# Later pools, four products ahead at a group boundary, one plain tile last, and another place for the forms of h, in a four-layer trunk

## The chip, the cores and the metric

The kernel runs on one core of a Trainium2 chip. The metric is the device time of one execution in microseconds (us); shown are the median of several runs and one profiled execution. TensorE is called PE, VectorE DVE, ScalarE ACT, GpSimd POOL; SP issues the transfers.

## The reference

A trunk of four post-norm layers on a sequence of 512 tokens of width 1024, all in float32. Each layer is a token mixer and a SwiGLU channel mixer (FFN) of 2816 hidden units:

```python
for i in range(DEPTH):
    x = sublayer(x, mixer[i % 4])      # mLSTM, sliding-window, HGRN2, differential attention
    x = sublayer(x, swiglu)            # (silu(h @ w_gate) * (h @ w_up)) @ w_out
# sublayer: h = x*(1+scale_c)+shift_c ; x = LayerNorm(alpha*x + (1+gate_c)*f(h))
```

The scale, shift and gate of each sub-layer are linear in one conditioning vector c.

## The kernel before

Activations lie transposed, features on the 128 partitions and 512 tokens in the free dimension; `xz` is the stream. A float32 product is made of three in the float32r type: each operand is split into a high part and the rest, and hi·hi, lo·hi and hi·lo are added in PSUM (`mm3`, L198 to L202; L502 for the Strassen products). A weight of 128 x 1024 is loaded into a `raw` buffer (L187), its high part `wh` is made by ACT (L190, L479) and the rest `wl` by DVE (L191, L480). `raw` has 7 buffers of 4 KB per partition, `wh` and `wl` 5 each, PSUM 8 banks.

The conditioning weights (`in_ada_w`, 192 loads of 512 KB) go through the same `raw` buffers. Each such column is one custom DVE instruction (L124). They are issued in between: each call of `weights` issues `rate` of them, unless `hold` counts down first (L192 to L195).

The FFN (L568 to L624) works in 22 hidden tiles of 128. Before, the first four are plain: their gate and up products use h itself (`hh`, `hl`). Between them `t_forms` (L458 to L473) makes four tiles `tf` of sums of h's blocks, which need the four blocks `H` in float32. The other 18 tiles are 9 pairs, each by one level of Strassen: seven products of 24 matmuls of 256 columns, on sums of weight blocks made in `raw` (L516, L542). Results are gathered by L513 to L564 and gated: silu and product by L528 and L554, split into `pair` by ACT (L555) and DVE (L556). After groups of 8, 8 and 6 hidden tiles comes an output projection of that group (`out_proj`, L322 and on): eight steps, one weight and one PSUM bank each, folded into `xz` by DVE (L337). The last one of a sub-layer runs its last four steps in two halves of the tokens, and the layer norm of the first half runs beside the second: sums S (L342 to L348), mean and variance by PE and DVE (L381, L388 to L398), scaling (L408, L416), then the next h (L444 ACT, L447 POOL, L448 DVE).

Each stage has its own pools in the memory that the stage before gives back: `tf`, `pairs` and `mid` for an FFN, `big` and `mid` for a mixer (`pools`, L66 to L74). Before, `run` opens them ahead of the generator of the stage. The code is a set of generators; the framework puts each engine's instructions into one fixed order when the kernel is built, by priority in the order of the code and by when it reckons inputs and buffers to be free. An engine works its own order strictly.

Addresses in a partition, from the built program: `wh` and `wl` lie at 1216 modulo 2048, `hh` and `hl` at 704, `tf` at 1216; all of these, and `pair`, at 64 modulo 128.

Of the kernel before, what the change touches and what calls it, by code (L numbers as in the profile page):

```python
# [19 lines left out]
P = 128  # L20
D = 1024
# [6 lines left out]
FGROUPS = (8, 8, 6)  # L28
FPLAIN = 4
# [13 lines left out]
class Trunk:  # L43
# [22 lines left out]
    def pools(self, kind):  # L66
# [368 lines left out]
    def modulate(self, z, hs, hb, k, t, eng=None):  # L435
# [3 lines left out]
        else:  # L439
            x = (k // 4, t.start // 256)  # L440
            if x not in self.keep:
                self.keep[x] = self.raw.tile([P, 4, 256], F32, tag="raw", name=self.nm("H"))
            h = self.keep[x][:, k % 4, :]
# [124 lines left out]
    def ffn(self, layer, gate):  # L568
# [12 lines left out]
        acts = []  # L581
        src = lambda j: [a["ffn_in"][layer, j, :, x, :] for x in range(2)]
# [7 lines left out]
        for x in (pa, pb):  # L590
            acts += [x[:, :, 0, :], x[:, :, 1, :]]
        n = (KF - FPLAIN) // 2
        steps = [None] * n

        def begin(i):
            if i < n:
                act = self.pair_tile()
                steps[i] = self.strassen(a["ffn_dp"][layer, i], forms, act), act
                next(steps[i][0])

        ends, j0 = np.cumsum(FGROUPS), 0
        begin(0)
        next(steps[0][0])
        for i in range(n):
            g, act = steps[i]
            for s in range(5):
                if s == 3:
                    begin(i + 1)
                if s == 4 and i + 1 < n:
                    next(steps[i + 1][0])  # L610
                next(g)
                yield 0.0
            acts += [act[:, :, 0, :], act[:, :, 1, :]]
            gn = len(acts)
            if j0 + gn in ends:
                srcs = [a["ffn_out"][layer, d, :, j0 * P : (j0 + gn) * P] for d in range(KD)]
                self.rate = 2
                if j0 + gn == KF:
# [238 lines left out]
    def swa(self, layer, gate):  # L857
        nc, a = self.nc, self.a
# [585 lines left out]
```

## Time and profile before

| | before |
|---|---|
| median of 3 runs | 2512.93 us (2512.45 to 2520.49) |
| the profiled execution | 2519.93 us, span 2517.9, mean granted clock 0.981 |
| PE busy | 2407.0 us, 96% of the span |
| DVE busy | 1811.3 us, 72% |
| PE waiting for ACT's first splits (L190) | 38.8 us in 6 times, 13.1 of it at the start |
| PE waiting for ACT's `pair` (L555) | 22.4 us in 9 times |

A row of the timeline is start, length, engine, line, operation, output and inputs, count, and in brackets the idle time before with what ended it. A row of the windows gives the window, its length, then busy time and count for PE, PE's weight loads, DVE, ACT and POOL, the granted clock, the transfers' share and GB/s. The four steps from a mixer to its FFN lie at about 244, 795, 1499 and 2141 us, the three from an FFN to the next mixer at 600 to 650, 1160 to 1200 and 1860 to 1900. The fourth FFN has no conditioning columns beside it.

### The profile page before, as it was taken

Reading aid. Unit: us, or ns where it says so; the run is one execution under the profiler, and the core shown is the slowest. Engines: PE = TensorE matmul, PEld = TensorE weight load, DVE = VectorE, ACT = ScalarE, POOL = GpSimd, SP = SyncE. Lnnn points to the kernel's source line nnn. Section 1 sums busy time; section 2 is a strip of 40 time slices with the busy share of each in tenths; the row PEclk is TensorE's granted clock in tenths of the full one; section 3 lists DMA queues with packets and bytes.
Section 4 is the critical chain, followed back from the end, with each engine's and each line's share of the span. In section 5 each row is a group of like instructions: output and inputs, shape, how many; then the busy total and the mean of one; then the engine's idle time right before and its main releaser. Section 6 shows DMA issues by size and latency. Waiting matters only on the chain.

```text
span 2517.9 us, 39980 instructions
## 1 busy us (share of the span) xinstructions
PE 2407.0 (96%) x15416; PEld 2148.6 (85%) x15416; DVE 1811.3 (72%) x3137; ACT 1104.9 (44%) x1917; POOL 476.9 (19%) x714
## 2 busy tenths in 40 slices
PE   7998999999998999997999989999989999899998
PEld 5777989898768989897888889898978888899997
DVE  6956887878786887877655567878785556866665
ACT  3543534343653635343433335343436554544443
POOL 5003100004334000006433331000042223200002
PEclk9999999999998999998999999999999999999999
DMA  8831373736210363744221103736362210332321
GB/s 311 291 127 42 118 243 92 243 101 201 76 35 26 118 234 92 243 142 151 84 68 60 51 29 123 234 99 237 117 196 85 66 43 26 109 118 84 118 80 47
DMA packets 93998, 312.31 MB, mean 124 GB/s; under 512 B 10736, under 2 KB 13168, under 8 KB 93808
## 3 DMA queue, kind: packets, MB, share of 16 engines
q1 hardware_dynamic: 92800, 309.43, 37.9%
q8 instruction: 121, 1.98, 0.3%
q14 instruction: 69, 0.57, 0.1%
q10 hardware_dynamic: 1008, 0.32, 0.1%
HBM read 307.62 MB, written 2.10 MB: 123 GB/s over the span
## 4 chain that ended last, share of the span: by engine, by line
PE 73%; DVE 13%; DMA 6%; issue 3%; POOL 2%; ACT 2%; ACTq 0%; DVEq 0%; POOLq 0%; SPq 0%
PE ps L502 18%; PE ps L200 15%; PE ps L202 15%; PE ps L201 15%; DMA raw<-in_ada_w 4%; DVE raw L124 3%; DVE wl L191 3%; DVE wl L480 2%; PE ps L1209 1%; PE ps L1043 1%; PE ps L905 1%; ACT wh L190 1%; PE ps L1270 1%; PE ps L1071 1%; DVE xz L408 1%
## 5 line engine op out<-in xcount | busy, mean ns | idle before, releaser
L479 ACT ACTIVATE wh<-raw 128x1024 fp32r<-128x1024 f32 x252 | 267.0, 1061 | 424.3 <-PE ps L502 161.6
L502 PE MATMUL ps<-tf,wh 128*128 128x256 f32 x2304 | 418.3, 283 | 0.5 <-ACT b L513 0.5
L190 ACT ACTIVATE wh<-raw 128x1024 fp32r<-128x1024 f32 (+1 forms) x251 | 256.1, 1029 | 318.0 <-PE ps L201 114.3
L480 DVE TENSOR_TENSOR wl<-raw,wh 128x1024 fp32r<-128x1024 f32 x252 | 307.6, 1223 | 110.7 <-ACT wh L479 110.6
L191 DVE TENSOR_TENSOR wl<-raw,wh 128x1024 fp32r<-128x1024 f32 (+1 forms) x251 | 302.5, 1212 | 110.2 <-ACT wh L190 92.0
L502 PEld LDWEIGHTS ps<-tf,wh 128*128 128x128 f32 x2304 | 359.8, 192 | 2.9 <-ACT b L513 2.3
L502 PE MATMUL ps<-tf,wl 128*128 128x256 f32 x1152 | 326.0, 283 | 0.0
L200 PE MATMUL ps<-pair,wh 128*128 128x512 f32 (+1 forms) x800 | 295.1, 370 | 22.4 <-ACT pair L555 22.4
L201 PE MATMUL ps<-pair,wh 128*128 128x512 f32 (+1 forms) x800 | 294.1, 369 | 0.0
L202 PE MATMUL ps<-pair,wl 128*128 128x512 f32 (+1 forms) x800 | 293.3, 368 | 0.0
L124 DVE CUSTOM_DVE_ANT_0 raw<-raw,cond,adab 128x1024 f32<-128x1024 f32 x192 | 255.7, 1344 | 48.6 <-DMA raw<-in_ada_w 48.5
L200 PE MATMUL ps<-hh,wh 128*128 128x256 f32 (+1 forms) x616 | 213.6, 352 | 38.4 <-ACT wh L190 37.6
L200 PE MATMUL ps<-wh,hh 128*128 128x512 f32 (+1 forms) x608 | 241.1, 399 | 6.5 <-ACT hh L444 5.1
L502 PE MATMUL ps<-hh,wl 128*128 128x256 f32 x864 | 244.5, 283 | 0.0
L502 PE MATMUL ps<-hl,wh 128*128 128x256 f32 x864 | 244.5, 283 | 0.0
L502 PE MATMUL ps<-hh,wh 128*128 128x256 f32 x864 | 244.5, 283 | 0.0
L337 DVE SCALAR_TENSOR_TENSOR xz<-ps,gate,xz 128x512 f32<-128x512 f32 (+1 forms) x208 | 129.6, 625 | 148.2 <-PE ps L202 147.4
L201 PE MATMUL ps<-wl,hh 128*128 128x512 f32 (+1 forms) x608 | 222.7, 366 | 1.7 <-DVE wl L191 1.6
L202 PE MATMUL ps<-wh,hl 128*128 128x512 f32 (+1 forms) x608 | 222.1, 365 | 0.6 <-DVE hl L448 0.6
L502 PEld LDWEIGHTS ps<-tf,wl 128*128 128x128 f32 x1152 | 221.1, 192 | 0.0
L201 PE MATMUL ps<-hl,wh 128*128 128x256 f32 (+1 forms) x616 | 212.8, 348 | 6.5 <-DVE hl L448 6.3
L202 PE MATMUL ps<-hh,wl 128*128 128x256 f32 (+1 forms) x616 | 213.4, 350 | 5.3 <-DVE wl L191 5.3
(290 smaller groups left out, 4978.2 us busy)
## 6 DMA issues: line engine op xcount, KB each, us to landing
raw<-in_ada_w SPq DMA_DIRECT2D x192, 512.0 KB, 4.7
raw<-in_ffn_dp SPq DMA_DIRECT2D x144, 512.0 KB, 3.7
raw<-in_ffn_out SPq DMA_DIRECT2D x64, 512.0 KB, 3.7
raw<-in_ffn_in SPq DMA_DIRECT2D x32, 512.0 KB, 3.9
raw<-in_ffn_out SPq DMA_DIRECT2D x32, 384.0 KB, 3.5
raw<-in_m_vo SPq DMA_DIRECT2D x16, 512.0 KB, 5.6
raw<-in_h_qf SPq DMA_DIRECT2D x16, 512.0 KB, 3.6
raw<-in_h_ig SPq DMA_DIRECT2D x16, 512.0 KB, 3.8
```

Source lines behind the costliest of these rows:

```text
L124: self.nc.vector.tensor_tensor_reduce(w, w, self.cond, 1.0, self.adab[:, sub, j : j + 1], ALU.mult, ALU.add, mod[:, j : j + 1])
L190: nc.scalar.activation(hi[:, :n], raw[:, :n], AF.Copy)
L191: (eng or nc.vector).tensor_tensor(lo[:, :n], raw[:, :n], hi[:, :n].bitcast(F32), ALU.subtract)
L200: nc.tensor.matmul(ps, lhs[0], rhs[0], start=start, stop=False)
L201: nc.tensor.matmul(ps, lhs[0], rhs[1], start=False, stop=False)
L202: nc.tensor.matmul(ps, lhs[1], rhs[0], start=False, stop=stop)
L337: nc.vector.scalar_tensor_tensor(z, ps[:, t], gate[:, d : d + 1], z, ALU.mult, ALU.add)
L408: V.tensor_tensor(z, z, st[:, 0, :], ALU.subtract)
L479: nc.scalar.activation(hi, raw, AF.Copy)
L480: nc.vector.tensor_tensor(lo, raw, hi.bitcast(F32), ALU.subtract)
L502: nc.tensor.matmul(ps[:, j * 256 : j * 256 + 256], w[a][:, c], m[b], start=first and j == k == a == b == 0, stop=k == 3 and a == 1, skip_g ...
L905: nc.tensor.matmul(ps, qTs[j][:, q], kz[:, :, k0 : k0 + nk * P], start=True, stop=True)
```

## The change

1. FGROUPS becomes (7, 8, 7). Three plain tiles stand at the head of an FFN; the fourth is the last hidden tile, made on PE between and behind the last pair's last products, and gated into a tile of its own.
2. At a group boundary two more products of the next pair run ahead of the output projection, four in all. The next pair's four loaded blocks keep four of the seven `raw` buffers through it.
3. The pools of a stage open inside the stage's generator: after 16 steps (the first half) of the FFN's first projection, after 7 or 8 steps of a mixer's. The mixers' rope tables and masks are issued behind that.
4. The four blocks `H` are allocated ahead of the mixer's last output projection; each gets a memset of one column on POOL.
5. `hold` is 8 for every stage but the first: no column is issued with its first eight weights.
6. In the FFN's memory the pairs come first, then 64 bytes (`off`, one memset), then `tf` and `mid`. `tf` is then at 0 modulo 128, `wh` and `wl` at 64.

The arithmetic is the same. 48 matmuls of 512 columns become 96 of 256, 64 weights of 1024 or 768 columns become 64 of 896; the loads are the same in number. POOL gets 20 memsets.

```diff
-FGROUPS = (8, 8, 6)
-FPLAIN = 4
+FGROUPS = (7, 8, 7)
+FPLAIN = (0, 1, 2, KF - 1)
...
         if kind == "ffn":
-            self.tf, self.pairs, self.mid = pool("tf", 4), pool("pairs", 4), pool("mid", 7)
+            self.pairs, off = pool("pairs", 4), pool("off", 1)
+            self.nc.gpsimd.memset(off.tile([P, 16], F32, name=self.nm("off")), 0.0)
+            self.tf, self.mid = pool("tf", 4), pool("mid", 7)
...
-        pa, pb = self.pair_tile(), self.pair_tile()
-        yield from self.proj_cols(
+        first = self.proj_cols(
             src(0) + src(1), "t", lambda ps: (gated(pa, 0, ps[0], ps[1]), gated(pa, 1, ps[2], ps[3]))
         )
+        for _ in range(2 * KD):
+            yield next(first)
+        self.pools("ffn")
+        pa, pb = self.pair_tile(), self.pair_tile()
+        yield from first
+        forms = self.t_forms()
         yield from self.proj_cols(src(2), None, lambda ps: gated(pb, 0, *ps))
-        forms = self.t_forms()
-        yield from self.proj_cols(src(3), None, lambda ps: gated(pb, 1, *ps))
...
+        cur = begin(0)
+        self.advance(cur[0], 2)
+        left = 5
         for i in range(n):
-            g, act = steps[i]
-            for s in range(5):
-                if s == 3:
-                    begin(i + 1)
-                if s == 4 and i + 1 < n:
-                    next(steps[i + 1][0])
-                next(g)
-                yield 0.0
+            g, act = cur
+            self.advance(g, left - 2)
+            yield 0.0
+            nxt = begin(i + 1) if i + 1 < n else None
+            if nxt:
+                self.advance(nxt[0], 1)
+            else:
+                last(0)
+            self.advance(g, 1)
+            if nxt:
+                self.advance(nxt[0], 1)
+            self.advance(g, 1)
+            yield 0.0
             acts += [act[:, :, 0, :], act[:, :, 1, :]]
+            if nxt is None:
+                last(1)
+                pc = self.pair_tile()
+                gated(pc, 0, *bank)
+                acts.append(pc[:, :, 0, :])
+            cur, left = nxt, 5
             gn = len(acts)
             if j0 + gn in ends:
...
+                self.advance(nxt[0], 2)
+                left = 3
                 yield from self.out_proj(srcs, 1, acts, gate, False)
...
     def swa(self, layer, gate):
         nc, a = self.nc, self.a
+        first = self.proj_tok(a["s_q"][0], 512, lambda *x: qdone(*x))
+        for _ in range(KD - 1):
+            yield next(first)
+        self.pools("mix")
         self.rope_tables()
...
-            if i:
-                self.pools(kind)
             gen = getattr(self, kind)(layer, gate)
...
-            self.rate, self.hold = 2 if kind == "mlstm" else 1, 0
+            self.rate, self.hold = 2 if kind == "mlstm" else 1, 8 if i else 0
...
-            self.keep = {} if more and plan[i + 1][0] == "ffn" else None
+            self.keep = None
+            if more and plan[i + 1][0] == "ffn":
+                blocks = [(x, y) for y in range(2) for x in range(2)]
+                self.keep = {b: self.raw.tile([P, 4, 256], F32, tag="raw", name=self.nm("H")) for b in blocks}
+                for x in self.keep.values():
+                    self.nc.gpsimd.memset(x[:, 0, 0:1], 0.0)
             out = self.out_proj(srcs, per, acts, gate, True)
```

Lines of the changed kernel are four or five higher up to the FFN: a split at L190 is L194 there, L444 is L445, L337 is L341, L124 is L128, L516 is L517, L554 to L556 are L555 to L557.

ACT at the first step from a mixer to its FFN. `sq` are the squares for the norm, `hh` the new h, `wh` the splits of the FFN's first weights. Before:

```order
L346 ACTIVATE sq_2045<-xz 128x256
L444 ACTIVATE hh<-xz,hb_1707,hs_1706 128x256 x2
L346 ACTIVATE sq_2072<-xz 128x256
L190 ACTIVATE wh_2097<-raw_2095 128x1024
L444 ACTIVATE hh<-xz,hb_1707,hs_1706 128x256
L190 ACTIVATE wh_2103<-raw_2101 128x1024
L190 ACTIVATE wh_2109<-raw_2107 128x1024
L190 ACTIVATE wh_2115<-raw_2113 128x1024
L444 ACTIVATE hh<-xz,hb_1707,hs_1706 128x256
```

After; one more split, of the first weight, stands ahead of all the squares, nine rows further up:

```order
L347 ACTIVATE S<-xz 128x256
L194 ACTIVATE wh_2096<-raw_2094 128x1024
L350 ACTIVATE sq_1917<-xz 128x256
L350 ACTIVATE sq_1947<-xz 128x256
L194 ACTIVATE wh_2102<-raw_2100 128x1024
L350 ACTIVATE sq_1965<-xz 128x256
L445 ACTIVATE hh<-xz,hb_1707,hs_1706 128x256
L350 ACTIVATE sq_1995<-xz 128x256
L194 ACTIVATE wh_2108<-raw_2106 128x1024
L445 ACTIVATE hh<-xz,hb_1707,hs_1706 128x256 x2
L350 ACTIVATE sq_2023<-xz 128x256
L194 ACTIVATE wh_2419<-raw_2417 128x1024
```

The splits moved from behind the last square to between the squares. Further down, not shown, the second weight of the third tile stands in the new order behind the four copies that make `tf`; before, there was a split ahead of these copies.

DVE at the first group boundary. `pair` is the pair that the coming output projection uses last, the rows on `raw` and `mod` are conditioning columns, `wl` the splits of its weights. Before:

```order
L124 ISA raw_3152,mod_2091<-raw_3152,cond,adab 128x1024
L124 ISA mod_2091 128x1
L556 TENSOR_TENSOR pair_2706<-b_434_2738,pair_2706 128x2x256
L191 TENSOR_TENSOR wl_3146<-raw_3143,wh_3145 128x1024
L516 TENSOR_TENSOR b_459_2967<-ps_3006,b_459_2967 128x512
L191 TENSOR_TENSOR wl_3184<-raw_3181,wh_3183 128x1024
L124 ISA raw_3187,mod_2091<-raw_3187,cond,adab 128x1024
L124 ISA mod_2091 128x1
L516 TENSOR_TENSOR b_447_2872<-ps_2878,b_447_2872 128x512
L124 ISA raw_3190,mod_2091<-raw_3190,cond,adab 128x1024
L124 ISA mod_2091 128x1
L554 SCALAR_TENSOR_TENSOR b_447_2872<-b_453_2932,b_447_2872 128x512
```

After:

```order
L557 TENSOR_TENSOR pair_2648<-b_427_2680,pair_2648 128x2x256
L517 TENSOR_TENSOR b_452_2909<-ps_2948,b_452_2909 128x512
L195 TENSOR_TENSOR wl_3106<-raw_3103,wh_3105 128x896
L128 ISA raw_3138,mod_2086<-raw_3138,cond,adab 128x1024
L128 ISA mod_2086 128x1
L517 TENSOR_TENSOR b_440_2814<-ps_2820,b_440_2814 128x512
L128 ISA raw_3141,mod_2086<-raw_3141,cond,adab 128x1024
L128 ISA mod_2086 128x1
L555 SCALAR_TENSOR_TENSOR b_440_2814<-b_446_2874,b_440_2814 128x512
L195 TENSOR_TENSOR wl_3135<-raw_3132,wh_3134 128x896
L557 TENSOR_TENSOR pair_2648<-b_440_2814,pair_2648 128x2x256
```

Of the columns that stood between the gathering of the last pair and its gating, two are left; the first gating stands ahead of them.

DVE at the last output projection of the first FFN, around the first half's folds (128x256) and the norm's sums S. Before:

```order
L337 SCALAR_TENSOR_TENSOR xz<-ps_5325,gate_1705,xz 128x512
L191 TENSOR_TENSOR wl_5702<-raw_5699,wh_5701 128x1024
L337 SCALAR_TENSOR_TENSOR xz<-ps_5385,gate_1705,xz 128x256
L124 ISA raw_5976,mod_2092<-raw_5976,cond,adab 128x1024
L124 ISA mod_2092 128x1
L337 SCALAR_TENSOR_TENSOR xz<-ps_5409,gate_1705,xz 128x256
L124 ISA raw_5985,mod_2092<-raw_5985,cond,adab 128x1024
L124 ISA mod_2092 128x1
L337 SCALAR_TENSOR_TENSOR xz<-ps_5433,gate_1705,xz 128x256
L337 SCALAR_TENSOR_TENSOR xz<-ps_5457,gate_1705,xz 128x256
L347 TENSOR_TENSOR S<-S,xz 128x256
L348 TENSOR_TENSOR S<-S,sq_5477 128x256
```

After:

```order
L341 SCALAR_TENSOR_TENSOR xz<-ps_5308,gate_1705,xz 128x512
L195 TENSOR_TENSOR wl_5655<-raw_5652,wh_5654 128x1024
L341 SCALAR_TENSOR_TENSOR xz<-ps_5371,gate_1705,xz 128x256
L341 SCALAR_TENSOR_TENSOR xz<-ps_5398,gate_1705,xz 128x256
L341 SCALAR_TENSOR_TENSOR xz<-ps_5425,gate_1705,xz 128x256
L341 SCALAR_TENSOR_TENSOR xz<-ps_5452,gate_1705,xz 128x256
L351 TENSOR_TENSOR S<-S,xz 128x256
L352 TENSOR_TENSOR S<-S,sq_5475 128x256
L341 SCALAR_TENSOR_TENSOR xz<-ps_5479,gate_1705,xz 128x256
L392 TENSOR_SCALAR lns_5511<-ps_5506 128x2
L351 TENSOR_TENSOR S<-S,xz 128x256
L393 TENSOR_TENSOR lnv_5512<-lns_5511 128x2
```

The columns are gone from between the folds. Eight that stood from the last group's gating to the norm's end come behind the norm, in the mixer. On POOL, the masks of the third mixer stand ahead of the sums S of the norm before it, and their first memset waits for the last Strassen product; before, they stood among the rows of h.

More of the change, by code (lines that the diff above doesn't have):

```diff
@@ L439, in modulate @@
         else:
[L440 to L443, printed above, removed]
+            h = self.keep[k // 4, t.start // 256][:, k % 4, :]
         nc.scalar.activation(
@@ new lines, in ffn, with last @@
+        yield from first
+        forms = self.t_forms()
+        yield from self.proj_cols(src(2), None, lambda ps: gated(pb, 0, *ps))
+        acts = [pa[:, :, 0, :], pa[:, :, 1, :], pb[:, :, 0, :]]
+        n = (KF - len(FPLAIN)) // 2
+        ends = np.cumsum(FGROUPS)
+        j0 = 0
+        bank = []
+        def last(x):
+            w = self.weights(src(3)[x], D)
+            ps = self.bank()
+            for k in range(KD):
+                self.mm3(
+                    ps,
+                    [y[:, k * P : (k + 1) * P] for y in w],
+                    [self.hh[:, k, :], self.hl[:, k, :]],
+                    k == 0,
+                    k == KD - 1,
+                )
+            bank.append(ps)
@@ L870, in swa, with qdone, proj_q @@
         qTs, acts = [], []
[L872 to L880 removed]
+        qts = []
+        def qdone(tt, ps):
+            q = self.b2([P, T])
+            self.rope(q, ps, tt, 8)
+            qts.append(q)
+        def proj_q(proj):
+            yield from proj
+            qt = qts[-NTT:]
             for jj in range(2):
@@ L950, in attend @@
             yield from self.pipeline(us, (0, 5, 6))
-        yield from proj_q(0)
+        yield from proj_q(first)
         yield from self.proj_tok(a["s_kv"], 256, kv)
@@ L959, in swa @@
             nc.scalar.activation(kz[r, h, :], ps[r, :], AF.Copy)
-        fill = proj_q(1)
+        fill = proj_q(self.proj_tok(a["s_q"][1], 512, qdone))
         for _ in range(1):
@@ L971, in diff @@
         nc, a = self.nc, self.a
+        first = self.proj_tok(a["d_qk"][0], 512, lambda *x: qkdone(*x))
+        for _ in range(KD - 1):
+            yield next(first)
+        self.pools("mix")
         self.rope_tables()
@@ L997, in flip, with qkdone @@
             return ps
-        def proj(g):
-            qk = []
-            def qkdone(tt, ps):
-                x = self.b2([P, T])
-                self.rope(x, ps, tt, 8)
-                qk.append(x)
-            yield from self.proj_tok(a["d_qk"][g], 512, qkdone)
+        qks = []
+        def qkdone(tt, ps):
+            x = self.b2([P, T])
+            self.rope(x, ps, tt, 8)
+            qks.append(x)
+        def proj(g):
+            yield from self.proj_tok(a["d_qk"][g], 512, qkdone) if g else first
+            qk = qks[-NTT:]
             v = self.b4([P, NTT, 256])
@@ L1105, in hgrn @@
         NH, NL = 8, 7
+        begun = self.proj_cols(
+            [a["h_qf"][i, x] for i in range(2) for x in range(2)], "t", lambda ps: (qfdone(0, *ps[:2]), qfdone(1, *ps[2:]))
+        )
+        for _ in range(KD):
+            yield next(begun)
+        self.pools("mix")
         masks = c.tile([P, NL, P], U8, tag="mcB", name="hmasks")
@@ L1284, in then @@
                 yield from x
-        yield from proj_qf(0)
+        yield from begun
         for g in range(4):
```

61 lines of the change are left out of this document (20 added, 41 removed).

## The prediction

> **What bounds the kernel now.** I read the busy shares first, then what PE waited for, then the stretches round the largest waits. From the page and from the list of PE's waits (engine, what it waited for, total us, times, longest):
>
> ```profile
> PE 2407.0 (96%) x15416; PEld 2148.6 (85%) x15416; DVE 1811.3 (72%) x3137; ACT 1104.9 (44%) x1917; POOL 476.9 (19%) x714
> PE ps L200 <- ACT wh L190: 38.8, 6, 13.1
> PE ps L200 <- ACT pair L555: 22.4, 9, 3.5
> ```
>
> PE is the bound, and the change takes no product away, so only time in which PE stands still or runs slowly can be won. The two waits are the places that the change touches: the first weights of an FFN, and the group boundaries inside it. The first place, in four windows of 14 us, one for each step from a mixer to its FFN (columns as in the header row):
>
> ```profile
> core 0: us, PE busy (x) PEld busy (x) DVE busy (x) ACT busy (x) POOL busy (x), PEclk, DMA share, GB/s
> 243.00:257.00 14.00, 7.21 (x36) 6.49 (x34) 11.81 (x24) 7.74 (x12) 5.67 (x7) 0.63 0.15 46
> 795.00:809.00 14.00, 7.22 (x34) 6.49 (x32) 11.71 (x24) 7.65 (x12) 5.68 (x7) 0.65 0.18 58
> 1499.00:1513.00 14.00, 7.22 (x34) 6.49 (x32) 11.48 (x23) 7.42 (x12) 5.68 (x7) 0.63 0.18 56
> 2140.00:2154.00 14.00, 7.21 (x35) 6.49 (x33) 12.09 (x25) 7.82 (x12) 5.74 (x8) 0.65 0.16 50
> ```
>
> Some 35 products of 256 columns ran in 14 us; at their steady 0.12 us (rows further down) they need 4.2. So each step loses 9.8 us, 39 in all. About 6.8 is PE idle, the rest the lower clock after it. Why it waits, from ACT's and SP's timelines (start, length) and the transfers of 188 to 212 us (median us to landing):
>
> ```profile
> 250.54 2.94 ACT L190 ACTIVATE wh<-raw 128x1024 fp32r<-128x1024 f32 x3
> 189.83 16.55 SPq L187 DMA_DIRECT2D raw<-in_ffn_in  x4
> raw<-in_ffn_in SPq DMA_DIRECT2D x4, 512.0 KB, 4.7
> ```
>
> The four weights were issued from 189.83 to 206.4 and land some 4.7 us later; ACT splits three of them after 250.54, because the splits stand behind the layer norm in ACT's order, as the order above has it. No transfer is late.
>
> **Mixer to FFN, part by part.** The pools now open after the first projection's first half, so the first split stands ahead of the first square and the next three among the LN's rows. PE can go on at once. What follows is bounded by DVE, whose work is the same:
>
> ```profile
> 244.00:250.00 6.00, 0.28 (x1) 0.29 (x2) 5.85 (x17) 3.96 (x7) 3.69 (x6) 0.69 0.00 0
> 250.00:256.00 6.00, 5.33 (x23) 4.81 (x24) 4.96 (x5) 3.45 (x4) 1.47 (x1) 0.50 0.26 81
> 256.00:262.00 6.00, 6.00 (x51) 6.00 (x51) 1.35 (x7) 0.00 (x0) 0.71 (x1) 0.95 0.55 184
> 262.00:272.00 10.00, 10.00 (x85) 10.00 (x85) 9.40 (x25) 9.06 (x15) 6.36 (x8) 1.00 0.01 2
> 272.00:282.00 10.00, 10.00 (x71) 9.39 (x70) 9.93 (x10) 9.44 (x12) 0.00 (x0) 1.00 0.36 108
> 282.00:292.00 10.00, 10.00 (x45) 8.26 (x44) 10.00 (x11) 5.54 (x8) 0.00 (x0) 1.00 0.82 312
> ```
>
> From 244 to 292 DVE worked 41.5 of 48 us. If PE runs ahead there, it meets DVE's second half of the norm, the forms of h and the first Strassen sums. DVE can move forward by no more than its idle 6.5 us; some of that must stay, since the second half's mean still comes from PE. I take 4 per FFN, 16 in all. The ends: 0 (the stall only moves), and 39 (all of PE's loss). The plain tile that leaves the head (48 products of 0.227, 10.9 us) is moved to the end, not removed.
>
> [...] In the new order ACT makes the third tile's second weight after all four copies of the forms, a pause that I estimate at 4 us. [...]
>
> **Group boundaries.** DVE's and PE's timelines and the window at the first boundary:
>
> ```profile
> 348.00:352.00 4.00, 2.74 (x13) 1.92 (x11) 4.00 (x7) 1.75 (x3) 0.00 (x0) 1.00 0.88 250
> 350.25 1.27 DVE L124 CUSTOM_DVE_ANT_0 raw<-raw,cond,adab 128x1024 f32<-128x1024 f32 x1
> 351.45 0.69 DVE L554 SCALAR_TENSOR_TENSOR b<-b,b 128x512 f32<-128x512 f32 x1
> 352.86 0.50 PE L200 MATMUL ps<-pair,wh 128*128 128x512 f32 x1 [2.12 <-ACT pair L555]
> 353.79 1.28 DVE L124 CUSTOM_DVE_ANT_0 raw<-raw,cond,adab 128x1024 f32<-128x1024 f32 x1
> ```
>
> The output projection runs out of finished tiles: the last pair's gating (L554, L555, L556) is queued on a full DVE behind 1.27 us columns. The change puts two more Strassen products there, 2 x 24 x 0.12 = 5.8 us of PE work, against a longest wait of 3.5. In the new order the pair's first gating stands ahead of every column, and two instead of four stand ahead of the last. All nine waits, 22.4 us, should close; the added splits and sums for two products (1.22 each) also come earlier, so I take 21. Ends: 12 (half left) and 22.4.
>
> **FFN to mixer.** Three windows, and two DVE rows in them:
>
> ```profile
> 600.00:650.00 50.00, 42.50 (x227) 36.55 (x227) 39.55 (x106) 24.76 (x42) 26.29 (x35) 0.90 0.33 104
> 1160.00:1200.00 40.00, 29.13 (x185) 27.73 (x184) 26.20 (x66) 12.38 (x20) 26.68 (x53) 0.79 0.30 94
> 1860.00:1900.00 40.00, 32.69 (x171) 27.47 (x170) 34.92 (x92) 21.76 (x36) 20.06 (x29) 0.91 0.33 99
> 604.79 1.60 DVE L124 CUSTOM_DVE_ANT_0 raw<-raw,cond,adab 128x1024 f32<-128x1024 f32 x1 [2.33 <-DMA raw<-in_ada_w]
> 1180.80 0.48 DVE L448 TENSOR_TENSOR hl<-h,hh 128x256 fp32r<-128x256 f32 x1 [4.88 <-POOL h L447]
> ```
>
> PE is idle 7.5, 10.9 and 7.3 us there, 25.7; the lower clock costs up to 10%, 21% and 9% of the windows, 5.0 + 8.4 + 3.6 = 17.0. Ceiling 42.7. Two causes show: a column that waits for its transfer while the folds and sums stand behind it (2.33 us at 604.79), and, in the second, POOL busy with masks while DVE waits 4.88 for h. The change holds the columns back for eight weights, and puts rope tables and masks ahead of the folds (masks wait for the last Strassen product, so they start before the out-projection). I leave a third, 4 to 5 us per place for the chain of the mean, and take 29. Ends 15 and 42.7.
>
> **What it costs.** About 25 columns of the three FFN ends go into the mixers:
>
> ```profile
> L124 DVE CUSTOM_DVE_ANT_0 raw<-raw,cond,adab 128x1024 f32<-128x1024 f32 x192 | 255.7, 1344 | 48.6 <-DMA raw<-in_ada_w 48.5
> 1200.00:1300.00 100.00, 98.73 (x626) 86.13 (x625) 59.56 (x115) 40.79 (x81) 39.61 (x62) 1.00 0.21 65
> ```
>
> 25 x 1.344 = 34 us of DVE. The cover is the mixer's own PE work, beside which DVE is busy 59.6 of 100 us. But nine of them come in a block right behind the norm, where others wait. I take 8; ends 0 and 34. The 48 products of 512 columns that become 96 of 256 add a fixed part each. PE's timeline gives it (first and last of a run; with the page's two groups of products that use a form):
>
> ```profile
> 306.16 0.28 PE L502 MATMUL ps<-tf,wl 128*128 128x256 f32 x1
> 306.88 0.28 PE L502 MATMUL ps<-tf,wl 128*128 128x256 f32 x1
> 347.63 0.39 PE L200 MATMUL ps<-pair,wh 128*128 128x512 f32 x1
> 350.12 0.39 PE L202 MATMUL ps<-pair,wl 128*128 128x512 f32 x1
> L502 PE MATMUL ps<-tf,wh 128*128 128x256 f32 x2304 | 418.3, 283 | 0.5 <-ACT b L513 0.5
> L502 PE MATMUL ps<-tf,wl 128*128 128x256 f32 x1152 | 326.0, 283 | 0.0
> ```
>
> Six products of 256 columns lie between the first two rows, eleven of 512 between the next two: 0.72 / 6 = 0.120 us and 2.49 / 11 = 0.226 us from start to start, so 2 x 120 - 226 = 14 ns are fixed, and 48 more products cost 0.7 us. The last plain tile's gating (about 3 us of ACT and DVE steps) has the last group's first six tiles to hide behind, 6 x 3 x 0.12 = 2.2 us in the halves; I take 0.5 us per FFN, 2 in all, ends 0 and 8. The 20 small memsets lie on POOL, 19% busy: nothing. The 64-byte offset of the forms I cost at nothing: forms and h lie 512 bytes apart modulo 2048, and all their products show the one pace; the other end stands with the rivals.
>
> **Sum.** 16 + 21 + 29 - 8 - 0.7 - 2 = 55 us off the profiled execution, 2519.93, so 2464.5. That execution lies 7 us above the median of the runs; off the median 2512.93 it is **2458 us**. The likeliest case's own range, from half of each doubtful term, is 2435 to 2485.
>
> **Rivals.**
> 1. The stalls move instead of going (0.16). For it: DVE's fullness from 262 to 292. Heads 0, boundaries 18, FFN ends 20, columns -17: 21 us, 2492.
> 2. The offset changes PE's pace (0.10). Modulo 128 bytes all operands of the large products lie at one place before, so no row shows what another place does. If the fixed 14 ns were a clash of the two reads, the 3456 products with forms would lose them: 47 us more, 2411. [...]
> 3. Starved out-projections, slower (0.08). Four raw buffers now hold the next pair's blocks during two out-projections of each of three FFNs; three are left for a weight and two columns per step. Issues of this stretch (345 to 400 us), median to landing:
>
> ```profile
> raw<-in_ada_w SPq DMA_DIRECT2D x8, 512.0 KB, 4.8
> raw<-in_ffn_out SPq DMA_DIRECT2D x4, 512.0 KB, 5.2
> ```
>
> With 1.3 us to consume it, a buffer turns in 6.2 to 6.5 us, and so do three; PE needs 21 x 0.227 = 4.76 us per step in the group of seven, 5.45 in that of eight. In the new order five weights stand ahead of the first fold. If only three of them are in time, five steps of each out-projection are exposed, and a turn of c costs 3 x 5 x (2c - 10.2) us. At 6.2 it would eat 33 of the 55; from c = 6.9 it eats all; at 8, 87 us: 2545. Against: with all five in time the sixth weight is wanted 5 x 4.76 = 24 us after the start, and six more transfers at a third of 6.5 us each need 13.
> 4. The change does not do what it says (0.10): the gating still waits behind columns, the added columns take back the rest, 2513.
>
> **Numbers.** The forecast's case 0.56. Faster takes that, the first two rivals and a part of the fourth: 0.85. Within 0.3%, 2505.4 to 2520.5, about what a measurement of this kernel can tell from nothing: 0.06. Slower: the third and a rest of the fourth, 0.09. Range 2418 to 2502: it takes in most of rivals 1 and 2.
>
> **What would show it.** PE's wait for pair at the gating line gone from its list; no half clock behind the mixer, and the first 256-column products at 0.12 us right behind the last out-projection; a new wait of PE for the third tile's weight, 3 to 5 us; the three FFN ends with PE over 90% busy; out-projection steps at 4.76 and 5.45 us. Steps of over 6 us show rival 3; products with forms under 0.12 us rival 2. The forecast is wrong if the mixers lose more than 15 us, or the heads gain nothing.

## The result, and the profile after

The changed kernel takes 2442.25 us (median of 4 runs, 2440.67 to 2445.28); the kernel before 2514.51 us in the runs beside it. The ratio is 0.971, 95% interval 0.969 to 0.973: 72 us less, where 55 were forecast. The profiled executions took 2519.93 and 2442.43 us, 77.5 apart; the terms below are of these two.

The busy times of the page, after:

```profile
PE 2379.4 (97%) x15464; PEld 2122.7 (87%) x15464; DVE 1795.5 (74%) x3137; ACT 1103.4 (45%) x1917; POOL 477.9 (20%) x734
```

PE has 48 more products and is busy 27.6 us less, for its clock drops less often (mean granted clock 0.996 after 0.981) and the steps of the products with forms are shorter (117.8 ns from start to start after 120.0). The list of PE's waits, after (total us, times, longest):

```profile
PE ps L204 <- ACT wh L194: 20.3, 6, 13.3
PE ps L205 <- DVE pair L557: 1.6, 2, 1.1
PE ps L503 <- ACT wh L480: 2.8, 4, 0.7
```

The wait for the first splits is down from 38.8 to 20.3 us, 13.3 of it at the start, 13.1 before; the wait for `pair` from 22.4 to 1.6. The four steps from a mixer to its FFN, in windows of the same length and place:

```profile
243.00:257.00 14.00, 12.67 (x98) 11.62 (x97) 11.77 (x29) 4.89 (x9) 6.43 (x9) 1.00 0.24 74
775.00:789.00 14.00, 12.66 (x98) 11.63 (x96) 12.20 (x29) 5.49 (x11) 6.95 (x10) 1.00 0.18 58
1449.00:1463.00 14.00, 12.66 (x97) 11.61 (x97) 11.72 (x29) 4.90 (x9) 6.44 (x9) 1.00 0.25 74
2071.00:2085.00 14.00, 12.66 (x98) 11.62 (x97) 11.71 (x29) 4.89 (x9) 6.47 (x9) 1.00 0.26 83
```

98 products instead of 36, and the clock stays at 1.00. The three steps from an FFN to the next mixer, each window with the same distance to the last product of the output projection as in the prediction:

```profile
581.30:631.30 50.00, 47.59 (x291) 41.71 (x290) 37.49 (x97) 26.61 (x43) 26.40 (x37) 0.97 0.26 78
1120.30:1160.30 40.00, 38.55 (x309) 37.01 (x308) 31.66 (x76) 20.71 (x34) 20.03 (x26) 1.00 0.24 78
1792.90:1832.90 40.00, 37.52 (x216) 32.11 (x215) 32.42 (x84) 22.40 (x38) 19.14 (x27) 0.96 0.21 67
```

PE is idle 2.4, 1.5 and 2.5 us there, after 7.5, 10.9 and 7.3 before, and so busy 94 to 96% of each.

To divide the gain, each matmul's time to the start of the next was compared with the common one of its shape and operands in the same trace (the 40th percentile), and the excess summed by stretch, in us. "Head" runs from the last product of the mixer to the first Strassen product, "end" from the last Strassen product to the mixer's first product of its own kind. "Pace" is the sum of the common times. "Boundaries" are the first two of an FFN; its third, between the last Strassen product and the last output projection, lies in "end". The runs named here are told below.

```
                         before  after | early  hlate  plain4  two    hold0
heads (4)                 43.1   21.6  | 21.8   51.4   25.5    21.9   21.6
pairs and boundaries      22.9    4.8  |  5.9    2.4    4.1    25.1    6.6
ends (4)                  57.8   24.0  | 24.3   23.4   44.8    21.3   43.1
start and mixers          51.4   54.6  | 55.5   56.5   53.2    57.3   51.2
pace                    2320.3 2312.8  | 2312.0 2312.0 2310.9  2312.0 2312.6
```

So the heads gave 21.5 us, the boundaries 18.1, the ends 33.8 and the pace 7.5; the mixers took 3.2. The sum is 77.7. Of the ends' 33.8, 0.9 is the fourth FFN's, which has no mixer behind it (4.6 to 3.7).

The kernel before was timed again beside each group of the experiments and took 2516.83, 2515.13 and 2518.64 us there. So differences of up to some 4 us between kernels of different groups say nothing, and the ratio to the kernel before is given with each time.

### The profile page after: what moved, and what is told of

Same layout as the page of the kernel before. It is cut to its first block, busy times and chain, and to the rows that moved or that the text cites. A ratio compares the mean times of both kernels' runs of the same rounds, so it can differ in the third digit from the quotient of the medians.

```text
span 2440.7 us, 40054 instructions
## 1 busy us (share of the span) xinstructions
PE 2379.4 (97%) x15464; PEld 2122.7 (87%) x15464; DVE 1795.5 (74%) x3137; ACT 1103.4 (45%) x1917; POOL 477.9 (20%) x734
## 4 chain that ended last, share of the span: by engine, by line
PE 81%; DVE 8%; ACT 3%; POOL 2%; DMA 2%; issue 2%; ACTq 0%; POOLq 0%; DVEq 0%; SPq 0%
PE ps L503 28%; PE ps L204 14%; PE ps L206 14%; PE ps L205 14%; DVE wl L195 2%; DMA raw<-in_ada_w 1%; PE ps L1250 1%; PE ps L1084 1%; DVE raw L128 1%; PE ps L941 1%; POOL H L448 1%; DVE xz L412 1%; DVE hl L449 1%; DVE xz L420 1%; ACT wh L194 1%
## 5 line engine op out<-in xcount | busy, mean ns | idle before, releaser
L194 ACT ACTIVATE wh<-raw 128x1024 fp32r<-128x1024 f32 (+1 forms) x251 | 257.8, 1030 | 379.2 <-DMA raw<-in_ffn_out 115.3
L503 PE MATMUL ps<-tf,wh 128*128 128x256 f32 x2304 | 410.8, 280 | 0.0
L195 DVE TENSOR_TENSOR wl<-raw,wh 128x1024 fp32r<-128x1024 f32 (+1 forms) x251 | 303.7, 1212 | 98.6 <-ACT wh L194 84.9
L503 PEld LDWEIGHTS ps<-tf,wh 128*128 128x128 f32 x2304 | 353.1, 188 | 0.9
L128 DVE CUSTOM_DVE_ANT_0 raw<-raw,cond,adab 128x1024 f32<-128x1024 f32 x192 | 246.7, 1296 | 47.0 <-DMA raw<-in_ada_w 46.3
L341 DVE SCALAR_TENSOR_TENSOR xz<-ps,gate,xz 128x512 f32<-128x512 f32 (+1 forms) x208 | 129.9, 625 | 160.2 <-PE ps L206 159.8
L204 PE MATMUL ps<-hh,wh 128*128 128x256 f32 (+1 forms) x616 | 207.1, 342 | 21.7 <-ACT wh L194 19.1
L205 PE MATMUL ps<-hl,wh 128*128 128x256 f32 (+1 forms) x616 | 207.5, 339 | 0.2
```

The costliest lines, as they stand in the source:

```text
L128: self.nc.vector.tensor_tensor_reduce(w, w, self.cond, 1.0, self.adab[:, sub, j : j + 1], ALU.mult, ALU.add, mod[:, j : j + 1])
L194: nc.scalar.activation(hi[:, :n], raw[:, :n], AF.Copy)
L195: (eng or nc.vector).tensor_tensor(lo[:, :n], raw[:, :n], hi[:, :n].bitcast(F32), ALU.subtract)
L204: nc.tensor.matmul(ps, lhs[0], rhs[0], start=start, stop=False)
L205: nc.tensor.matmul(ps, lhs[0], rhs[1], start=False, stop=False)
L341: nc.vector.scalar_tensor_tensor(z, ps[:, t], gate[:, d : d + 1], z, ALU.mult, ALU.add)
```

## The experiments

**What made the head's gain: pools, or buffers of h.** Two kernels undo one part each. `early` opens each stage's pools ahead of its generator again:

```diff
+            if i:
+                self.pools(kind)
             gen = getattr(self, kind)(layer, gate)
...
-        for _ in range(2 * KD):
-            yield next(first)
-        self.pools("ffn")
```

> The changed kernel with part 3 undone for the pools alone: each stage's pools open ahead of its generator, as before. Theory A (the late pools put the first splits ahead, and with them the head's gain): PE waits again some 6 us for the first split at each of the four steps from a mixer to its FFN, with half clock behind; PE's loss at the heads goes from 5.4 back to 10 to 12 us each, 20 us or more in all, median near 2463 or above. Rival B (the other parts, above all the plain tile that left the head, made the gain): the heads lose 5 to 6 us each as now, median under 2450.

Measured: 2444.53 us (2443.95 to 2446.06), 0.9714 of before (0.9686 to 0.9741), where the changed kernel has 0.971: no difference that can be told. Its first window at a head:

```profile
243.00:257.00 14.00, 12.68 (x98) 11.63 (x97) 11.90 (x29) 5.00 (x10) 6.44 (x10) 1.00 0.23 71
```

98 products, as in the changed kernel. The late pools are not what brought the head its gain. `hlate` undoes part 4: the blocks of h take their buffers inside the norm.

```diff
-                self.keep = {b: self.raw.tile([P, 4, 256], F32, tag="raw", name=self.nm("H")) for b in blocks}
-
-                for x in self.keep.values():
-                    self.nc.gpsimd.memset(x[:, 0, 0:1], 0.0)
+                self.keep = {}
...
-            h = self.keep[k // 4, t.start // 256][:, k % 4, :]
+            x = (k // 4, t.start // 256)
+            if x not in self.keep:
+                self.keep[x] = self.raw.tile([P, 4, 256], F32, tag="raw", name=self.nm("H"))
+            h = self.keep[x][:, k % 4, :]
```

> The changed kernel with part 4 undone: the four blocks of h take their raw buffers as the norm writes them, as before. Theory A (the early buffers put the first splits among the norm's rows, since opening the pools early lost nothing): in the built order the four splits stand behind the last square again, so PE waits 6 us for the first split at each head, with half clock behind: 10 to 12 us lost per head in place of 5.4, about 22 in all, median near 2464. Rival B (the head's gain has another cause, such as the held columns): under 5 us.

Measured: 2470.14 us (2468.5 to 2473.41), ratio 0.9812 (0.9793 to 0.9832), 28 us above the changed kernel; the heads lose 51.4 us, 8 more than before the change. PE waits 6.1 us for the first split at each head again, and in addition 2.2 us for a split (L195) further on in the plain tiles, a wait that the kernel before did not have. ACT's timeline at the first head of `hlate`:

```profile
248.53 1.04 ACT L194 ACTIVATE wh<-raw 128x1024 fp32r<-128x1024 f32 x1
250.44 2.94 ACT L194 ACTIVATE wh<-raw 128x1024 fp32r<-128x1024 f32 x3
```

Its list of PE's waits, and its window at that head:

```profile
PE ps L204 <- ACT wh L194: 38.8, 6, 13.1
PE ps L206 <- DVE wl L195: 14.4, 15, 2.2
```

```profile
243.00:257.00 14.00, 7.23 (x41) 6.50 (x40) 11.87 (x25) 7.64 (x12) 5.70 (x8) 0.76 0.16 52
```

The same rows of ACT in the changed kernel:

```profile
236.98 1.06 ACT L194 ACTIVATE wh<-raw 128x1024 fp32r<-128x1024 f32 x1 [0.17 <-PE ps L205]
240.92 1.06 ACT L194 ACTIVATE wh<-raw 128x1024 fp32r<-128x1024 f32 x1 [0.29 <-PE ps L205]
243.96 1.04 ACT L194 ACTIVATE wh<-raw 128x1024 fp32r<-128x1024 f32 x1
```

With the blocks allocated inside the norm the splits stand behind its last square, with the pools late or not. Part 4 carries the head. By what rule of the framework an allocation of `raw` moves the splits of other weights was not tried, so that step stays open.

**The plain tile.** `plain4` undoes part 1: groups of 8, 8 and 6, four plain tiles first.

```diff
-FGROUPS = (7, 8, 7)
-FPLAIN = (0, 1, 2, KF - 1)
+FGROUPS = (8, 8, 6)
+FPLAIN = (0, 1, 2, 3)
...
+        yield from self.proj_cols(src(3), None, lambda ps: gated(pb, 1, *ps))
...
-            else:
-                last(0)
...
-            if nxt is None:
-                last(1)
-                pc = self.pair_tile()
-                gated(pc, 0, *bank)
-                acts.append(pc[:, :, 0, :])
```

> The changed kernel with part 1 undone: groups 8, 8, 6 and four plain tiles at the head, none last; pools, four ahead, hold and the gap as changed. Theory A (DVE sets the head, and the plain tile took its two splits and its gating, some 3.8 us of DVE, away from it): the heads lose 3 to 4 us more each, 14 us in all, median near 2456. Rival B (the head's gain is the order alone): the heads lose 5.4 us as now, median 2440 to 2445.

Measured: 2463.18 us (2462.52 to 2464.15), ratio 0.9787 (0.9759 to 0.9815), 21 us more, and by neither theory: the heads lose only 3.9 us more, the ends 20.8. PE's waits in `plain4`:

```profile
PE ps L204 <- ACT pair L556: 8.5, 3, 3.3
PE ps L204 <- ACT hh L445: 8.0, 9, 2.1
PE ps L385 <- DVE S L351: 7.3, 2, 5.5
```

The third boundary of an FFN has no next pair whose products could cover the last gating. The tile that was moved to the end covers it: without it three waits of about 2.8 us are back, where the kernel before had three too. PE's timeline of the kernel before at these places:

```profile
583.29 0.50 PE L200 MATMUL ps<-pair,wh 128*128 128x512 f32 x1 [1.54 <-ACT pair L555]
1138.20 0.73 PE L200 MATMUL ps<-pair,wh 128*128 128x512 f32 x2 [2.79 <-ACT pair L555]
1838.22 0.73 PE L200 MATMUL ps<-pair,wh 128*128 128x512 f32 x2 [2.87 <-ACT pair L555]
```

These waits are 8.5 of the 20.8 us. The shorter last group also leaves less cover for the norm: at the second FFN's end PE waits 5.5 us for the sums S, which POOL makes there behind the third mixer's masks. The 3.9 us of the heads are mostly a lower clock (0.57 to 0.66) at two of the four: those lost 7.1 and 7.2 us, the other two 5.6, against 5.4 in the changed kernel.

**Four products ahead.** `two` undoes part 2, so that five `raw` buffers are free in the output projections.

```diff
-                self.advance(nxt[0], 2)
-                left = 3
```

> The changed kernel with part 2 undone: two products ahead at a group boundary instead of four, so five raw buffers are free in the output projection. Theory A (the two products cover the last pair's gating): PE waits again at the nine boundaries, 14 to 18 us more, median 2456 to 2460. Rival B (the regrouping and the order of the columns closed the waits): 2442. Rival C (four held raw buffers slow the output projections and take back a part): the boundaries come back, but the projections gain, net under 10 us, 2445 to 2450.

Measured: 2461.71 us (2460.83 to 2464.48), ratio 0.9783 (0.9749 to 0.9817), 19.5 us more. The stretch of pairs and boundaries loses 20.3 us more. This row of its list of waits is back:

```profile
PE ps L204 <- ACT pair L556: 11.0, 6, 3.6
```

The six waits lie at the first two boundaries of three FFNs, where the kernel before had six of its nine (15.2 us). So the two products are the cover, as theory A had it, but of six waits and not of nine; the other three are the plain tile's. The buffers that they hold cost nothing that shows: with three free, a step of these output projections takes 4.76 us in the groups of seven and 5.44 in those of eight, the first one 0.04 more, in all eight of them. In `two`, with five free, most steps take the same, and the first ones, where the waits are, 5.05 to 9.63.

**Held columns.** `hold0` undoes part 5.

```diff
-            self.rate, self.hold = 2 if kind == "mlstm" else 1, 8 if i else 0
+            self.rate, self.hold = 2 if kind == "mlstm" else 1, 0
```

> The changed kernel with part 5 undone (hold 0): columns are again issued with the first eight weights of a stage, so they stand between the last folds of an FFN. Theory A (the held columns made the gain from FFN to mixer): the stretches from the last output projection to the mixer's interior lose 15 to 20 us more over three FFNs, median near 2459; the mixers lose 3 us less. Rival B (rope tables and masks ahead of the folds made it): under 5 us more, 2442 to 2447.

Measured: 2459.61 us (2456.4 to 2464.21), ratio 0.9774 (0.9744 to 0.9804), 17.4 us more. The ends lose 19.1 us more, the mixers 3.4 less. PE's waits in `hold0`:

```profile
PE ps L385 <- DVE S L351: 11.0, 7, 3.0
PE ps L205 <- DVE pair L578: 5.7, 3, 2.2
```

The sums of the norm wait behind columns again, and so does the gating of the last plain tile (L578; 1.3 us in the changed kernel). Theory A held in its numbers. The five parts undone one by one add to 28 + 21 + 19.5 + 17 + 2 us, more than the 72 that all six give together: the parts lean on each other, and undoing one can open waits that the kernel before did not have, as in `hlate`.

**The gap of 64 bytes.** `nooff` leaves it out:

```diff
-            self.pairs, off = pool("pairs", 4), pool("off", 1)
-            self.nc.gpsimd.memset(off.tile([P, 16], F32, name=self.nm("off")), 0.0)
+            self.pairs = pool("pairs", 4)
             self.tf, self.mid = pool("tf", 4), pool("mid", 7)
```

> The changed kernel without the gap: pairs, forms and mid in that order, the forms at the weights' place modulo 256. Theory A2: products with forms at 120 ns, 3456 x 2.1 = 7 us more, median near 2450. Rival B (128 bytes gave 119 ns and 4 us, so the place modulo 128 is not what counts, and the pace belongs to the new order of the pools): 118 ns, 2442.

Measured: 2450.02 us (2447.42 to 2452.2), ratio 0.973 (0.9711 to 0.975): 7.8 us more by the medians, 5 by the ratios, whose intervals overlap. What shows the effect is the step. Products with forms in PE's timeline, `nooff` first, then the changed kernel; nine steps lie between the two rows of each:

```profile
293.15 0.28 PE L502 MATMUL ps<-tf,wl 128*128 128x256 f32 x1
294.23 0.28 PE L502 MATMUL ps<-tf,wl 128*128 128x256 f32 x1
```

```profile
292.43 0.28 PE L503 MATMUL ps<-tf,wl 128*128 128x256 f32 x1
293.49 0.28 PE L503 MATMUL ps<-tf,wl 128*128 128x256 f32 x1
```

1.08 / 9 = 0.120 us against 1.06 / 9 = 0.118. So between these two kernels the gap alone changed PE's pace: the sum of common times is 9.1 us longer in `nooff`. Two more gaps ask whether the place modulo 128 bytes decides:

```diff
-off.tile([P, 16], F32, ...)
+off.tile([P, 32], F32, ...)    # off128
+off.tile([P, 8], F32, ...)     # off32
```

> The changed kernel with 128 bytes of gap instead of 64, so that the forms lie again at the weights' place modulo 128; instructions the same. Theory A (the two reads of a product clash when both operands lie at the same place modulo 128 bytes): the products with forms go back from 118 to 120 ns from start to start, about 3456 x 2.2 ns = 7.6 us, median near 2450. Rival B (the pace went with the new order or with where the pool ends, not with the place modulo 128): the pace stays 118 ns and the median 2442.

> The changed kernel with a gap of 32 bytes: forms at 96 modulo 128, weights at 64. If the clash is between two 64-byte halves, 32 bytes change part of the steps: a pace between 118 and 120 ns, or 120 as with no gap. If any difference of place is enough, 118 ns. Rival B: 118 as well, whatever the gap. Told by the steps in the profile, not by the time.

Measured: 2446.49 us with 128 bytes (2442.45 to 2447.49; ratio 0.9709, 0.9691 to 0.9726), and 2444.39 in the one run with 32. The mean step of products with forms is 118.9 ns with 128 bytes, spread from 115 to 122, and 117.8 with 32. So the place modulo 128 is not what told the paces apart: 0 and 128 bytes agree in it and gave 120.0 and 118.9. `before_off` adds the gap, and the pairs first, to the kernel before:

```diff
-            self.tf, self.pairs, self.mid = pool("tf", 4), pool("pairs", 4), pool("mid", 7)
+            self.pairs, off = pool("pairs", 4), pool("off", 1)
+            self.nc.gpsimd.memset(off.tile([P, 16], F32, name=self.nm("off")), 0.0)
+            self.tf, self.mid = pool("tf", 4), pool("mid", 7)
```

> The kernel before with part 6 alone: pairs first, 64 bytes, then the forms. Theory A: products with forms at 118 ns, 7.6 us less than before: 2505 to 2507, ratio 0.997. Rival B: 120 ns, no difference.

Measured: 2515.17 us against 2516.83, ratio 0.999 (0.9977 to 1.0003): no difference that can be told. The pace came (118 ns, 8.9 us less in the sum of common times), and waits took it back:

```profile
PE ps L202 <- ACT pair L557: 24.8, 9, 3.3
PE ps L383 <- DVE S L349: 19.7, 4, 9.6
```

PE's wait for the norm's sums is 19.7 us, 10.9 before. But the edit changed more than the pace: the order that was built moved too. At the second FFN's end the third mixer's masks now stand ahead of the norm's sums on POOL. POOL in `before_off`, then the first such sum in the kernel before (its last Strassen product lies 1.8 us earlier):

```profile
1159.99 0.29 POOL L1118 CAST hmasks<-b 128x128 uint8<-128x128 f32 x1
1160.24 2.30 POOL L349 TENSOR_TENSOR S<-S,xz 128x512 f32<-128x512 f32 x1
```

```profile
1143.50 1.86 POOL L347 TENSOR_TENSOR S<-S,xz 128x512 f32<-128x512 f32 x1 [0.32 <-DVE xz L337]
```

That makes the wait of 9.6 us, 3.7 at this end before; in return PE's wait for `hl` falls from 6.3 us to 0.3. At the first and the third end the wait for the sums grew from 2.7 us to 4.3 and 4.1. There PE may simply arrive earlier at work that is bound by DVE and the columns; with a changed order that is not shown. By the stretches of the table, pairs and boundaries lose some 7 us more than in the kernel before, the ends 8, and the heads 4 less.

`wshift` moves the weights' splits by 64 bytes instead, so that every product with a weight is touched:

```diff
-        self.wp = pool("wp", 5)
+        for x in ("o1", "o2"):
+            tc.nc.gpsimd.memset(pool(x, 1).tile([P, 16], F32, name=x + "t"), 0.0)
+            if x == "o1":
+                self.wp = pool("wp", 5)
```

> The changed kernel without the gap at the forms, but with the weights' splits wh and wl moved by 64 bytes, so that every product with a weight (13320 matmuls) has its two operands 64 bytes apart modulo 128. Theory A: all of them gain some 2.2 ns, those of 256 columns go to 118 and those of 512 to about 224 ns; 13320 x 2.2 = 29 us in place of 7.6, median near 2421. Rival B: nothing is gained, and the forms' share is lost or kept: 2442 to 2450. Rival C (only the products of 256 columns gain, since the weight load lasts as long as they do): some 8500 x 2.2 = 19 us, 2431.

Measured: 2436.16 us (2434.73 to 2438.41), ratio 0.9672 (0.9655 to 0.9689). Products of 256 columns with h ran at 114 ns, but those of 512 columns at 233. PE's timeline, `wshift`, 20 steps between the rows, then the changed kernel, 17 steps:

```profile
271.12 0.39 PE L206 MATMUL ps<-hh,wh 128*128 128x512 f32 x1
275.78 0.39 PE L208 MATMUL ps<-hh,wl 128*128 128x512 f32 x1
```

```profile
272.50 0.39 PE L206 MATMUL ps<-hh,wl 128*128 128x512 f32 x1
276.35 0.39 PE L205 MATMUL ps<-hl,wh 128*128 128x512 f32 x1
```

4.66 / 20 = 0.233 us against 3.85 / 17 = 0.226: what won at one width lost at the other. Rival C comes nearest: the products of 256 columns gained, by 2 to 6 ns, but those of 512 lost instead of keeping theirs. Its ground, a weight load as long as the product, shows in the prediction's windows as busy time alone: from 262 to 272 us, in products of 256 columns, PE and its weight loads are each busy 10.00 us; from 282 to 292, in products of 512, 10.00 and 8.26. That this decides which width gains is not shown. The best distance seen was 192 bytes, so two kernels take it: `off192` for the forms alone, `hh192` for h as well.

```diff
-off.tile([P, 16], F32, ...)
+off.tile([P, 48], F32, ...)    # off192, hh192
...
+        self.nc.gpsimd.memset(self.state.tile([P, 48], F32, name="o1"), 0.0)    # hh192
         self.hh = self.state.tile([P, KD, T], F32R, name="hh")
         self.hl = self.state.tile([P, KD, T], F32R, name="hl")
+        self.nc.gpsimd.memset(self.state.tile([P, 16], F32, name="o2"), 0.0)    # hh192
```

> The changed kernel with a gap of 192 bytes, so that the forms lie 192 bytes behind the weights modulo 256. Theory A2 (the pace goes by the distance of the moving operand from the weights modulo 256: 0 gave 120 ns, 64 gave 118, 128 gave 119, 192 gave 114 for h against the moved weights): products with forms at 113 to 114 ns, 3456 x 4 = 14 us less than with 64, median near 2428. Rival B (what gave 114 there was h's own place, not the distance): 118 to 120 ns, 2442 to 2450.

> As the run with a gap of 192 bytes, and the high and low parts of h moved by 192 bytes as well, with 64 bytes behind them, so that all else keeps its place modulo 256. Theory A2: the 2592 Strassen products with h and the 960 of 256 columns at the heads go from 120 to 114 ns, 21 us less; the 888 products of 512 columns with h moving go from 227 to 233 ns and those with h as the loaded operand (1344) to 229, 5 + 3 us more; net 13 us below the run with the gap alone, near 2415. Rival B: no change beside that run.

`off192` measured 2432.36 us (2428.89 to 2433.67), ratio 0.9658 (0.9638 to 0.9677): 10 us under the changed kernel, 17.7 under `nooff` of the same group, and the fastest of all. `hh192` measured 2438.82 (2436.25 to 2443.55), ratio 0.9689 (0.9667 to 0.971), where 2415 was expected. Products with forms in the two, nine steps and 21 steps:

```profile
293.10 0.28 PE L503 MATMUL ps<-tf,wl 128*128 128x256 f32 x1
294.12 0.28 PE L503 MATMUL ps<-tf,wl 128*128 128x256 f32 x1
```

```profile
294.44 0.28 PE L505 MATMUL ps<-tf,wl 128*128 128x256 f32 x1
296.91 0.28 PE L505 MATMUL ps<-tf,wl 128*128 128x256 f32 x1
```

1.02 / 9 = 0.113 us and 2.47 / 21 = 0.118. In `hh192` forms and weights have the same distance as in `off192`, but both lie 256 bytes further. So in these runs the distance alone does not give the pace, and theory A2 falls in that form. Which places are best for which width stays open.

## Why the prediction came out

The time, 2442, lies in the range, 16 us under the forecast of 2458. By its steps:

- **Mixer to FFN: 16 forecast, 21.5 measured, for another cause.** The step that failed is "The pools now open after the first projection's first half, so the first split stands ahead of the first square". The order did show the splits ahead, but `early` shows that the late pools are not needed for it, and `hlate` that they are not enough without the early buffers of h. Only the place of the rows was read from the order, and from that the size came; which part put them there was guessed. The bound held: DVE's 6.5 us of idle time in the first head, of which 4.7 were gained. The moved tile's share is small: in `plain4` the two heads without a lower clock lose 0.2 us more each.
- **The pause at the third tile's second weight** came where it was put, at 1.45 us, and 0.70 more behind it, in place of 4. PE's timeline of the changed kernel:

```profile
278.42 0.50 PE L204 MATMUL ps<-hh,wh 128*128 128x512 f32 x1 [1.45 <-ACT wh L194]
278.76 0.39 PE L205 MATMUL ps<-hl,wh 128*128 128x512 f32 x1
279.85 0.58 PE L503 MATMUL ps<-hh,wh 128*128 128x256 f32 x1 [0.70 <-ACT wh L480]
```

  The new order puts the first two Strassen products among this weight's products, and they wait 0.70 us for a split of their own, which I had not seen. The windows over the pause and behind it, in the first FFN and in the second:

```profile
276.00:280.00 4.00, 1.85 (x8) 0.91 (x6) 4.00 (x5) 4.00 (x6) 0.00 (x0) 0.93 0.65 170
280.00:284.00 4.00, 4.00 (x13) 3.23 (x14) 3.97 (x5) 0.74 (x1) 0.00 (x0) 0.64 0.90 316
808.50:812.50 4.00, 1.83 (x8) 0.87 (x6) 4.00 (x5) 4.00 (x6) 0.00 (x0) 1.00 0.54 150
812.50:816.50 4.00, 3.94 (x17) 3.16 (x18) 3.97 (x5) 0.88 (x1) 0.00 (x0) 1.00 0.93 310
```

  The two pauses, 2.15 us of waiting among 1.85 us of work, were followed by a lower clock in the first FFN alone: 13 products in four microseconds at 0.64, against 17 at 1.00 in the second. In all four FFNs the two waits are the same within 0.02 us. The forecast of 16 counts no lower clock behind them. In the kernel before PE waited 6.1 us for the first split at each of the four heads, and the clock was 0.50 behind every one (windows of 6 us from 250, 801, 1505 and 2146 us); behind these shorter pauses it was lower at one of four. Which place is hit differs between the profiled executions: with the same two pauses a lower clock (0.57 to 0.66) followed at the last three places in `two`, at the last two in `hold0` and at the first two in `plain4`. How long a pause has to be for it, and what picks the place, no run here shows.
- **Group boundaries: 21 forecast, 18.1 measured** (22.9 to 4.8), by the mechanism named for six of the nine waits. `two` gives 20.3 back when the two products go. "All nine waits, 22.4 us, should close" has a step that fails: the two products run ahead at the first two boundaries alone, with 15.2 us of the waits. The other three, 7.2 us, lie at the third boundary, where there is no next pair, in the stretch "ends" of the table. They closed too, but by the plain tile at the end.
- **FFN to mixer: 29 forecast, 33.8 measured** (57.8 to 24.0), between the bounds of 15 and 42.7; the measured stretch also holds the third boundary and the fourth FFN's end. The held columns carry it, as forecast: 19.1 in `hold0`. The other cause named, the masks put ahead of the folds, was not undone alone; PE's wait for `hl` (6.3 us before) is gone in the changed kernel and in `hold0` alike, so the hold did not close it, and in `before_off`, where the masks stand ahead as well, it is 0.3. But the forecast did not see a second carrier. It priced the plain tile at the end as a cost, "I take 0.5 us per FFN, 2 in all", because it counted only that tile's own gating; `plain4` shows that the tile's products cover the gating of the last pair (8.5 us of waits), and that the ends lose 20.8 us without it. The two shares together exceed the whole, so they cannot be added.
- **Mixers: 8 forecast as a loss, 3.2 measured.** With the hold undone the mixers win 3.4 us. The columns found room on DVE: in the 100 us behind the second FFN's end (1140 to 1240) it is busy 70.4 us, in `hold0` (1150 to 1250) 60.3.
- **PE's pace: priced at nothing, 7.5 us measured.** This is the second mis-sized term: "The 64-byte offset of the forms I cost at nothing: forms and h lie 512 bytes apart modulo 2048, and all their products show the one pace". That argument compared only places that agree modulo 256, so it could show nothing of a gap of 64. The products with forms (us busy, mean ns of one), first in `nooff`, then in the changed kernel:

```profile
L502 PE MATMUL ps<-tf,wl 128*128 128x256 f32 x1152 | 326.0, 283 | 0.0
```

```profile
L503 PE MATMUL ps<-tf,wl 128*128 128x256 f32 x1152 | 321.4, 279 | 0.0
```

  The row of `nooff` is the same to the last digit as the one quoted of the kernel before. Over 3456 products the step went from 120.0 to 117.8 ns, 7.6 us; `nooff` gives 5 to 8 us back.

**The rivals.** Rival 2 had the right kind of effect and the wrong size: 47 us against 7.5; its 2411 lies 7 us under the range. Its ground, a fixed 14 ns that a gap would remove, does not stand: the gap of 64 bytes took 2 ns, that of 192 took 6 (`off192`, 17.7 us under `nooff`). The shortest mean step of any group of 256 columns in these runs was 114 ns. That a clash of the two reads makes the difference was the author's supposition, and no run shows it; what the runs show is 2450.02, 2442.25 and 2432.36 us with gaps of 0, 64 and 192 bytes, at steps of 120.0, 117.8 and 114.1 ns in the products with forms. Rival 3, starved output projections, is not seen: the steps are 4.76 and 5.44 us, where the prediction wanted 4.76 and 5.45, and none is over 6. Rival 1 falls with the heads, which gave 21.5 us where it had nothing, and rival 4 with the boundaries (18.1) and the mixers, which took back only 3.2.

**The sum.** 16 + 21 + 29 - 8 - 0.7 - 2 = 55 was forecast. Measured, by profiled executions: 21.5 + 18.1 + 33.8 - 3.2 + 7.5 = 77.7. Of the 22 us between, 8.2 are the pace (7.5 that were priced at nothing, and the 0.7 of fixed parts, which the measured pace holds), 5.5 the heads and 4.8 the mixers. The rest is boundaries and ends, and there the line has to be drawn as in the table: of the 21 for nine waits, 14 belong to the first two boundaries and 7 to the ends. Then the boundaries gave 4 more than forecast, and the ends 33.8 against 29 + 7 - 2 = 34. That the ends agree so closely is luck in part: the plain tile, entered as a loss of 2, carries a share of what the hold and the masks were to give.

## What to carry to other kernels

An instruction order shows where a row has moved, not which edit moved it: the head's gain was put down to the pools and belongs to the buffers of h, so undo the parts one at a time before you say why. A faster pace of the bound engine is worth only what its waits leave of it: 8.9 us of pace gave a ratio of 0.999 in the kernel before, where the edit also moved other rows, and 5 to 8 us in the changed one, where most waits were gone. Before you call such an edit a test of the pace alone, compare the built orders. A short chain of another engine at a boundary is best covered by products of the next stage. When products of one shape show one pace everywhere, that says little until the places of their operands differ (114.1 to 120.0 ns here, at 256 columns); it is cheap to try some.

## What the runs showed of the hardware

In these runs PE's pace differed with the places of a product's two operands in a partition: 114.1 to 120.0 ns from start to start at 256 columns, 227 to 233 at 512. Mean steps in ns, steps with a wait or a lower clock left out, by the place of the moving operand minus that of the loaded one, modulo 256 bytes; the second column has both places modulo 512, from the built programs:

```
distance  places           256 columns   512 columns
0         192/192, 448/448    120.0        227
32        224/192             117.8
64        256/192, 320/256    117.8         229
128       320/192             118.9
192       384/192             114.1
192       192/256             114.1         233
192       128/448             117.7
192       384/448             116.8         233
```

The 512-column figures are of products with `pair` moving at 0 and 64, and with h moving at 192 (228 at 0). The row of 32 is one execution. Two things here were not expected. The width of 256 columns had its worst pace where that of 512 had its best (120.0 and 227 ns, at distance 0), so none of these places was best for both. And the distance alone did not decide: 192 bytes gave 114.1, 116.8 and 117.7 ns, although the rows 384/192, 384/448 and 128/448 agree even in both places modulo 256. What decides was not found in these runs.
